# The triangular solve of a DeltaNet stage kept on VectorE, with the steps around it placed anew

## The chip, the cores and the metric

The kernel runs on one core of a Trainium2 chip. The metric is the device time of one execution in microseconds. TensorE (PE; PEld its weight loads), VectorE (DVE), ScalarE (ACT), GpSimd (POOL) and SyncE (SP, which here only issues DMA transfers) run their own instruction streams and meet at semaphores. L282 means line 282 of the kernel before.

## The reference

One layer of a hybrid trunk, on 2048 prompt frames of one stream and on 8 sample streams of 16 frames, with a model width of 1024, all in float32:

```
h   = RMSNorm(x);  P = h @ w_in      -> q|k|v (3*512) | z 512 | b 4 | a 4 | B 512 | C 512 | H 512
A   (gated DeltaNet, 4 heads x 128): causal conv(4) + SiLU on q,k,v; l2norm q,k; beta = sigmoid(b)
    g = -exp(A_log) softplus(a + bias);  decay[i,j] = exp(G_i - G_j), i >= j, G = cumsum(g) in a chunk
    A = strict(beta k k^T * decay);  solve (I + A) [u | w] = [beta v | beta k exp(G)]   (unit lower triangular)
    v_new = u - w S;  o = (q exp(G)) S + (q k^T * decay) v_new;  S = S a_last + k_tail^T v_new
    o = RMSNorm_head(o) * SiLU(z)
B   (short conv): y = B * conv3(C * H)
x   = x + RMSNorm(concat(o, y) @ w_o);  x = x + RMSNorm(SwiGLU(RMSNorm(x)))
```

The order of frames binds two things: the convolution's history, and the state S from chunk to chunk. The sample streams bring their own states and depend on no prompt frame.

## The kernel before

Frames are cut into 17 tiles of 128: 16 of the prompt, and tile 16, the sample (8 streams of 16). Every float32 product is made of three matmuls of rounded halves (hi*hi, lo*hi, hi*lo), so a block of the w_in product with its eight k-slices takes 24 matmuls.

**Stage 1** runs to 1065 us. `GROUPS` (L31) orders the tiles in five groups of 3, 4, 4, 3 and 3. Each group goes through 28 *slots*, one for each 128 columns of w_in, in the order of `SEQ` (L40): k, q, two of v, z, two of v, then the C, H and B columns of the short convolution. A slot's 24 matmuls (L282) have up to 512 columns and are issued in three *thirds* (k 0 to 2, 3 to 5, 6 and 7), so 9, 9 and 6 matmuls. After a slot, `finish_block` (L338) reads the PSUM bank: copy (L290), convolution by multiply-adds on VectorE (L286, the "taps"), Silu on ScalarE (L319). For k, q and v a `later` is returned: the turn (transposition by TensorE, L326) of the Silu's output, which the loop at L902 issues at the end of the next slot.

Between thirds, `plan` (L749) places the steps of the DeltaNet at numbered thirds 0 to 83. It counts time with `THIRD`, an assumed length of a third, so `after(us)` is a number of thirds. In order: `gate_rates`, `gate_sums` and `gate_decay` make the cumulated decay, and gate_decay sends it through DRAM (`grow`) to be broadcast, adds the masks (L493) and takes the Exp; `key_norms`; `decay_scale` (L499); `pair_keys` (L511: four k k^T products into a `gbank`, times `dt`, into `AU`, L516); `pair_queries`; `solve_load`, `solve` in four parts, `solve_store`; `level_a` to `level_d`, which join the inverted 32x32 blocks to 128x128 by small matmuls; then the sample's heads or `chunk`, one thread of four steps per prompt tile, that updates S. The next group's x is brought in meanwhile: `x_rows` (sums of squares), `x_norm` (L233: load and scale), `x_split` (hi and lo, L207, L208), the last two k-slices behind the last slot (`next_rows`, L807).

**The triangular solve.** Each tile and head has four diagonal 32x32 blocks. `solve_load` (L525) writes them to DRAM (`sa`) and reads them so that one partition holds one whole block: 48 or 64 partitions, 1024 numbers each (`As`), with an identity in `Ts`. `solve` makes 31 steps, each a product of a column and a row (L546) and a subtraction (L548). `solve_store` writes the inverse (`sT`) and its turned copy (L553, `sU`) to DRAM and reads both back as `td` and `ud` (one tile, `utd`) with a block's rows over partitions. `level_a` starts with ScalarE copies of `ud` (L566) and matmuls on `td` (L573).

TensorE's order is that of the program text (`manual_schedule`, L815); the other engines' instructions are ordered by the framework's scheduler by its own cost model. `issue_after(x)` makes an instruction be issued behind x. SP's queue carries the loads of weights and x in order. In group 0 (and for a quarter of the blocks in group 1) weights come raw and are split: ScalarE rounds (L260), then VectorE or GpSimd subtracts (L262), and the split weights are written to DRAM (`wsplit`) for the later groups. PSUM has eight banks: three for blocks (`dbank`), two for turns (`tbank`), two for small products (`gbank`), one for outputs (`obank`).

**Then**, from L935, w_o is loaded and split, `o_tile` (L940, matmuls L958) makes the mixer's output tile by tile, and the feed-forward network follows (L1174, L1332).

```
            for slot, j in enumerate(SEQ):
                ...
                for s, ks in enumerate((range(0, 3), range(3, 6), range(6, 8))):
                    ...
                    for f in events.pop(3 * slot + s, ()):
                        f()
                while laters:
                    laters.pop()()
                if later:
                    laters.append(later)
```

## Time and profile before

| what | value |
|---|---|
| time, median of 3 runs (lowest to highest) | 2675.58 us (2666.0 to 2676.9) |
| profiled execution: time, span | 2681.41 us, 2679.5 us |
| granted TensorE clock, mean | 0.971 |
| busy: TensorE, VectorE, ScalarE, GpSimd | 2505.2, 1681.2, 981.9, 647.1 us |
| stage 1, windows from 7.57 to 1069.35 | 1061.78 us, TensorE busy 927.34 |

The page's first part gives each engine's busy time and share of the span; its PEclk line gives, for 40 equal slices, the granted clock in tenths of full speed. Windows are rows of "start:end length, busy time (number of instructions) of PE, PEld, DVE, ACT, POOL, granted clock, DMA share, GB/s". Rows of waits read "engine, its output and line <- engine, output and line that it waited for: us in total, times, longest". Rows of the timeline read "start, length, engine, line, operation, output <- inputs, shape, count", with the idle time before them in brackets. Rows of groups end in the total, the mean in ns, and the idle time before them by what ended it. Pieces of the chain of waits read "start, length, what".

### The profile page before, as it was taken

The page shows a single profiled execution, that of the slowest core. Times are in us where ns is not written, and L with a number is a line of the kernel's source. Part 1 is how long each engine was busy: PE and PEld are TensorE (multiplying, and loading weights), DVE is VectorE, ACT ScalarE, POOL GpSimd, SP SyncE. Part 2 cuts the span into 40 slices and gives each one's busy share as a digit, 9 for nine tenths or more (in the row PEclk, how much of TensorE's full clock was granted, in tenths as well). Part 3 has the DMA queues.
Part 4 walks back from the last instruction along what each step waited for, and adds up shares of the span by engine and source line. Part 5 has one row for each costly group of instructions (what it writes and reads, how often), then busy time and mean ns, then how long its engine had stood idle before and what let it go on. Part 6 is the DMA issues. An engine that isn't in the chain of part 4 may idle for free.

```text
span 2679.5 us, 39414 instructions
## 1 busy us (share of the span) xinstructions
PE 2505.2 (93%) x14366; PEld 2281.7 (85%) x14366; DVE 1681.2 (63%) x3081; ACT 981.9 (37%) x2090; POOL 647.1 (24%) x710
## 2 busy tenths in 40 slices
PE   6879989889898888999999999999999999999998
PEld 6777778668798788888999999999999988788876
DVE  5856655554473554585988884454655554677588
ACT  5433522522432522353443442222433335333343
POOL 2321101101010100021655630000000015555564
PEclk8989999999999999999999999999999999999999
DMA  5676555454566565666987888878888954333466
GB/s 199 210 240 205 172 197 192 148 156 171 177 217 210 172 201 183 204 214 218 334 290 261 267 282 264 266 250 257 278 279 282 288 174 129 118 121 122 132 202 189
DMA packets 314993, 567.28 MB, mean 212 GB/s; under 512 B 53564, under 2 KB 201216, under 8 KB 297776
## 3 DMA queue, kind: packets, MB, share of 16 engines
q1 hardware_dynamic: 184384, 487.32, 54.9%
q10 hardware_dynamic: 130416, 77.45, 9.5%
q8 instruction: 113, 1.85, 0.3%
q14 instruction: 80, 0.66, 0.1%
HBM read 402.65 MB, written 162.05 MB: 211 GB/s over the span
## 4 chain that ended last, share of the span: by engine, by line
PE 53%; DVE 6%; DMA 4%; issue 2%; ACT 1%; POOL 1%; ACTq 0%; SPq 0%; DVEq 0%; POOLq 0%
PE fbank L1174 30%; PE fbank L1332 12%; PE dbank L282 3%; PE tbank L958 3%; PE dbank L958 3%; DMA dr<-in_w_dn 1%; DVE acc L1291 1%; DMA partd<-pt 1%; POOL dw L1031 1%; DVE xr L1351 0%; PE ftbank L981 0%; DVE fw L1150 0%; DVE dw L1031 0%; DMA fh<-hTd 0%; DMA ru<-in_w_gu 0%
## 5 line engine op out<-in xcount | busy, mean ns | idle before, releaser
L1174 PE MATMUL fbank<-xh,fw 128*128 128x384 f32 (+1 forms) x3696 | 899.7, 327 | 7.6 <-ACT m L1208 4.0
L282 PE MATMUL dbank<-hi,w 128*128 128x384 f32 (+1 forms) x2240 | 691.2, 377 | 20.6 <-ACT hi L207 12.7
L1174 PEld LDWEIGHTS fbank<-xh,fw 128*128 128x128 f32 x3696 | 651.9, 188 | 9.4 <-ACT m L1208 4.7
L1174 PE MATMUL fbank<-xl,fw 128*128 128x384 f32 (+1 forms) x1848 | 603.0, 326 | 0.0
L282 PEld LDWEIGHTS dbank<-hi,w 128*128 128x128 f32 x2240 | 431.4, 196 | 60.4 <-ACT hi L207 15.1
L1332 PE MATMUL fbank<-dw,as 128*128 128x512 f32 x1980 | 462.3, 395 | 8.9 <-DVE as L1316 2.6
L1332 PEld LDWEIGHTS fbank<-dw,as 128*128 128x128 f32 x1980 | 373.0, 189 | 97.8 <-DVE acc L1291 4.0
L282 PE MATMUL dbank<-lo,w 128*128 128x384 f32 (+1 forms) x1120 | 414.0, 370 | 3.9 <-DVE lo L208 3.9
L1174 PEld LDWEIGHTS fbank<-xl,fw 128*128 128x128 f32 x1848 | 347.7, 188 | 0.0
L1316 POOL TENSOR_TENSOR as<-ar,as 128x256 fp32r<-128x256 f32 (+1 forms) x207 | 186.3, 911 | 282.6 <-ACT as L1313 281.9
L282 PEld LDWEIGHTS dbank<-lo,w 128*128 128x128 f32 x1120 | 220.1, 196 | 24.4 <-DVE lo L208 8.0
L1291 DVE TENSOR_TENSOR acc<-acc,fbank 128x512 f32<-128x512 f32 x248 | 166.4, 682 | 97.4 <-PE fbank L1332 79.6
L1031 POOL TENSOR_TENSOR dw<-dr,dw 128x512 fp32r<-128x512 f32 x52 | 77.3, 1498 | 484.5 <-ACT dw L1029 484.2
L1313 ACT CAST as<-ar 128x256 fp32r<-128x256 f32 (+1 forms) x288 | 118.4, 427 | 188.7 <-PE fbank L1332 134.7
L286 DVE SCALAR_TENSOR_TENSOR acc<-R,cw,acc 128x512 f32<-128x512 f32 (+2 forms) x180 | 122.4, 682 | 68.1 <-ACT acc L315 66.2
L1149 ACT CAST fw<-rg 128x512 fp32r<-128x512 f32 x124 | 77.4, 624 | 192.3 <-PE fbank L1174 148.5
L1221 DVE TENSOR_TENSOR c<-u,fbank 128x384 f32<-128x384 f32 (+1 forms) x66 | 34.9, 528 | 102.0 <-PE fbank L1174 101.9
L307 POOL COPY hist<-R 128x3 f32<-128x3 f32 x60 | 16.3, 271 | 282.8 <-ACT R L290 256.4
L1217 DVE TENSOR_TENSOR m<-m,m 128x384 f32<-128x384 f32 (+1 forms) x44 | 23.1, 526 | 94.5 <-ACT m L1210 94.4
L1219 ACT ACTIVATE m<-fbank 128x384 f32<-128x384 f32 (+1 forms) x66 | 31.3, 474 | 125.0 <-PE fbank L1174 115.8
L1150 POOL TENSOR_TENSOR fw<-rg,fw 128x512 fp32r<-128x512 f32 x44 | 69.6, 1582 | 30.2 <-ACT fw L1149 30.0
L260 ACT CAST w<-wr 128x512 fp32r<-128x512 f32 x70 | 40.3, 617 | 79.0 <-PE dbank L282 49.4
(341 smaller groups left out, 3572.3 us busy)
## 6 DMA issues: line engine op xcount, KB each, us to landing
w<-wsplit SPq DMA_DIRECT2D x105, 1024.0 KB, 5.0
fw<-fsplit SPq DMA_DIRECT2D x188, 512.0 KB, 4.9
fsplit<-fw SPq DMA_DIRECT2D x94, 512.0 KB, 4.2
partd<-pt ACTq DMA_DIRECT2D x88, 384.0 KB, 6.5
rg<-in_w_gu SPq DMA_DIRECT2D x62, 512.0 KB, 3.7
wsplit<-w SPq DMA_DIRECT2D x28, 1024.0 KB, 5.4
ar<-partd SPq DMA_DIRECT2D x48, 384.0 KB, 3.3
wr<-in_w_in SPq DMA_DIRECT2D x70, 256.0 KB, 4.8
```

What stands on the lines that cost most here:

```text
L260: A.copy(wh[:, c], wr)
L282: T.matmul(ps[:, :c], l[:, k, :], r[k][:, :c], start=(k == 0 and r is hi and l is wh), stop=(k == KD - 1 and l is wl))
L286: V.scalar_tensor_tensor(acc, raw(d), w[:, d:d + 1], acc, op0=ALU.mult, op1=ALU.add)
L958: T.matmul(pss[n], m_[:, j, :], w_[k][:, n * 512:(n + 1) * 512], start=(k == 0 and ci == 0), stop=(k == KD - 1 and ci == 2))
L1031: e.tensor_tensor(out=w[:, 1], in0=v, in1=w[:, 0].bitcast(F32), op=ALU.subtract)
L1149: A.copy(w[:, 0], v)
L1150: e.tensor_tensor(out=w[:, 1], in0=v, in1=w[:, 0].bitcast(F32), op=ALU.subtract)
L1174: T.matmul(ps, w_[:, c], b_[k][:, :hw], start=(first and k == 0 and ci == 0), stop=(k == KH - 1 and ci == 2), skip_group_check=not first)
L1291: V.tensor_add(dst, dst, ps)
L1313: ins = A.copy(a[:, 0, :n], v)
L1316: e.tensor_tensor(out=a[:, 1, :n], in0=v, in1=a[:, 0, :n].bitcast(F32), op=ALU.subtract)
L1332: T.matmul(ps, a[:, x_, q * P:(q + 1) * P], w[:, y_], start=(start and q == 0 and ci == 0), stop=(q == c - 1 and ci == 2), skip_group_chec ...
```

## The change

- The sample moves from the first group to the fourth; the groups' sizes stay 3, 4, 4, 3, 3. `x` transposed is laid out in the groups' order. In `SEQ`, all z columns come ahead of all v columns.
- The solve stays on the chip. `solve_load` gathers the diagonal blocks with four ScalarE copies into `pk`, and one VectorE transposition of 32x32 squares spreads them in `As` so that each block lies on two partitions, each of which holds one half of the inverse's columns (the even or the odd ones). `Ts` gets a constant half identity by one DMA. A step works on 128 partitions and on j // 2 + 1 columns where it had j + 1. `solve_store` makes `td` and `ud` with two VectorE transpositions. All transfers by `sa`, `sT` and `sU` are gone.
- The decay of all tiles is one buffer with one broadcast DMA; the masks are a step of their own, `decay_mask`, issued behind the taps issued latest (`mark["V"]`), with one Exp for all tiles. The sigmoid's Exp moves from `gate_rates` into `gate_sums`, next to the other Exps.
- `laters` are issued one third of a slot later: behind the first third of the slot after the next.
- `THIRD` and the distances in `plan` are changed; chunks begin at third 52 at the earliest (54 before), the sample's heads follow each other by 5 thirds (6 before).
- Loads of x are steps of their own (`x_rows_load`, `x_load`), ahead of the arithmetic; the slices for k = 6 and 7 have buffers of their own and are loaded at thirds 72 and 73.
- Of the second halves of the raw weights VectorE splits the first eight only, GpSimd the others.
- In the last group `ahead`, at third 64, loads two blocks of w_o and the first tile's mixer input into buffers that are free by then, and the first `o_tile` starts from them.

The diff, cut to its core. Where a function is listed above, lines taken out of it are left out here if the new ones replace them whole.

```diff
-GROUPS = [[0, 1, 16], [2, 3, 4, 5], [6, 7, 8, 9], [10, 11, 12], [13, 14, 15]]
+GROUPS = [[0, 1, 2], [3, 4, 5, 6], [7, 8, 9, 10], [11, 12, 16], [13, 14, 15]]
...
-THIRD = {3: 1.75, 4: 2.35}
+THIRD = {3: 1.95, 4: 2.5}
...
-SEQ = [*range(0, 4), *range(8, 12), 4, 5, *range(12, 16), 6, 7, *range(16, 28)]
+SEQ = [*range(0, 4), *range(8, 12), *range(12, 16), *range(4, 8), *range(16, 28)]
...
+    e = np.arange(512)[None, :]
+    c[:, 904:1416] = e // 16 == 2 * (e % 16) + i[:, None] // 16 % 2
...
-        def x_rows(tiles, i, nx):
+        def x_rows_load(tiles, i, nx):
             if not i:
                 nx["ss"] = small.tile([P, 2 * MAXT], F32, tag="xss", name="xss")
+            nx["xt"] = []
             for q in range(2):
+                xt = cp.tile([P, W1], F32, tag="x", name="xt")
                 with tc.issue_after(wloads[-1].ins):
                     nc.sync.dma_start(out=xt, in_=x[tiles[i], :, q * 512:(q + 1) * 512])
+                nx["xt"].append(xt)
+        def x_rows(i, nx):
+            for q, xt in enumerate(nx["xt"]):
                 acc = nx["ss"][:, q * MAXT + i:q * MAXT + i + 1]
+                with tc.issue_after(mark["V" if q else "A"].ins):
+                    if q:
+                        V.scalar_tensor_tensor(xt, xt, 1.0, xt, op0=ALU.mult, op1=ALU.mult, accum_out=acc)
+                    else:
+                        A.activation(xt, xt, AF.Square, accum_out=acc)
...
+        def x_load(tiles, k, nx):
+            c, (gi, _) = len(tiles) * P, PLACE[tiles[0]]
+            xk = xbuf() if k < KD - 2 else cp.tile([P, W1], F32, tag="x", name="xt")
+            o = sum(len(g) for g in GROUPS[:gi]) * P
+            with tc.issue_after(wloads[-1].ins):
+                nc.sync.dma_start(out=xk[:, :c], in_=xT[k, :, o:o + c])
+            nx["xk"].append(xk)
         def x_norm(tiles, k, nx):
+            c, xk = len(tiles) * P, nx["xk"][k]
+            with tc.issue_after(mark["V"].ins):
+                V.tensor_mul(xk[:, :c], xk[:, :c], nx["rb"][:, :c])
...
+        wlo = [0]
...
                 A.copy(wh[:, c], wr)
+                e = V if q and wlo[0] < 8 else G
+                wlo[0] += q
                 e.tensor_tensor(out=wl[:, c], in0=wr, in1=wh[:, c].bitcast(F32), op=ALU.subtract)
...
+            mark["A"] = A.activation(dst[:, :pc], acc[:, :pc], AF.Silu)
...
+                mark["A"] = A.activation(g["sz"][:, h, :c], src, AF.Silu)
...
+            gg = sm("gg")
...
             V.tensor_mul(v3(gg)[:, :n], sp3[:, :n, 4:8], nega.unsqueeze(1).broadcast_to([P, n, H]))
+            g["sp3"], g["gg"] = sp3, gg
...
             m = 4 * n
             V.tensor_scalar_mul(nG[:, :m], ps[:, :m], -1.0)
             V.tensor_add(tl[:, :m], ps[:, 64:64 + m], nG[:, :m])
+            with tc.issue_after(A.activation(tl[:, :m], tl[:, :m], AF.Exp).ins):
+                A.activation(eG[:, :m], ps[:, :m], AF.Exp)
+                A.activation(eL[:, :m], ps[:, 64:64 + m], AF.Exp)
+                if g["npr"] < n:
+                    g["eLs"] = sm("eLs", 4 * NS)
+                    A.activation(g["eLs"], ps[:, 128:128 + 4 * NS], AF.Exp)
+                sb = sm("sb")
+                A.activation(sb[:, :m].rearrange("p (t h) -> p t h", h=H), g["sp3"][:, :n, 0:4], AF.Exp, scale=-1.0)
+            g.update(nG=nG, eG=eG, tl=tl, eL=eL, beta=sb)
...
             nc.scalar.dma_start(out=grow[:m], in_=rw[:m])
...
+            g["dt"] = dt = gp.tile([P, MAXT, H, P], F32, tag="dt", name="dt")
+            nc.sync.dma_start(out=dt[:, :n].rearrange("p t h c -> p (t h) c"), in_=grow[:m].partition_broadcast(P))
+        def decay_mask(g):
+            dt, nG = g["dt"], g["nG"]
+            with tc.issue_after(mark["V"].ins):
+                for i, t in enumerate(g["tiles"]):
+                    for h in range(H):
+                        V.scalar_tensor_tensor(dt[:, i, h, :], dt[:, i, h, :], nG[:, 4 * i + h:4 * i + h + 1],
+                                               neg_s if t == SAMPLE else neg_p, op0=ALU.add, op1=ALU.add)
+            A.activation(dt[:, :g["n"]], dt[:, :g["n"]], AF.Exp)
         def decay_scale(g, i):
...
         def solve_load(g):
+            n = g["n"]
+            As, Ts = (wk.tile([P, NS * (P + LS)], F32, tag=nm, name=nm) for nm in ("As", "Ts"))
+            Ts = Ts[:, :512]
+            nc.sync.dma_start(out=Ts, in_=half_eye)
+            pk = wk.tile([P, H, P], F32, tag="kl", name="pk").rearrange("p h c -> p (h c)").rearrange("p (i x) -> p i x", i=32)
+            if n < MAXT:
+                G.memset(pk, 0.0)
+            if g["npr"] < n:
+                G.memset(U[:, g["npr"]], 0.0)
             for b in range(4):
                 r = slice(32 * b, 32 * b + 32)
+                A.copy(pk[r, :, :4 * n], AU[r, :n, :, r].rearrange("p t h i -> p i (t h)"))
+            As = As[:, :1024].rearrange("p (j i) -> p j i", j=32)
+            V.transpose(As.rearrange("p j i -> p i j"), pk.unsqueeze(2).broadcast_to([P, 32, 2, 4 * MAXT]))
+            g.update(As=As, Ts=Ts.rearrange("p (i c) -> p i c", i=32))
         def solve(g, js):
-            m, As, Ts = g["n"] * 16, g["As"], g["Ts"]
+            As, Ts = g["As"], g["Ts"]
             for j in js:
                 pr = wk.tile([P, 256], F32, tag="pr", name="pr")
-                a, b = 31 - j, j + 1
-                p3 = pr[:m, :a * b].rearrange("p (i c) -> p i c", c=b)
-                V.tensor_mul(p3, As[:m, j, j + 1:32].unsqueeze(2).broadcast_to([m, a, b]),
-                             Ts[:m, j, 0:b].unsqueeze(1).broadcast_to([m, a, b]))
-                V.tensor_sub(Ts[:m, j + 1:32, 0:b], Ts[:m, j + 1:32, 0:b], p3)
+                a, b = 31 - j, j // 2 + 1
+                p3 = pr[:, :a * b].rearrange("p (i c) -> p i c", c=b)
+                V.tensor_mul(p3, As[:, j, j + 1:32].unsqueeze(2).broadcast_to([P, a, b]),
+                             Ts[:, j, 0:b].unsqueeze(1).broadcast_to([P, a, b]))
+                V.tensor_sub(Ts[:, j + 1:32, 0:b], Ts[:, j + 1:32, 0:b], p3)
         def solve_store(g):
             utd = wk.tile([P, NS * (P + LS)], F32, tag="As", name="utd")
+            ud, td = (utd[:, 512 * q:512 * q + 512].rearrange("p (x c) -> p x c", c=32) for q in range(2))
+            V.transpose(td.rearrange("p x (k e) -> p k e x", e=2), g["Ts"].rearrange("p i c -> p c i"))
+            V.transpose(ud, td)
+            g.update(ud=ud.rearrange("p (t h) c -> p t h c", h=H), td=td.rearrange("p (t h) c -> p t h c", h=H))
...
-            third = THIRD[n]
+            third = THIRD[n] if gi else 2.3
...
-            at(5 + after(11), gate_sums, g)
-            at(5 + after(16), gate_decay, g)
-            tk = 15
-            at(tk, key_norms, g)
+            t = 5 + after(11)
+            at(t, gate_sums, g)
+            t += after(4.5)
+            at(t, gate_decay, g)
+            t = max(t + after(12), 17)
+            at(t, decay_mask, g)
+            at(17, key_norms, g)
+            t += after(6)
...
-                at(tk + after(3), decay_scale, g, i)
-                at(tk + after(7 + 2 * i), pair_keys, g, i)
+                at(t - 1, decay_scale, g, i)
+                at(t + after(2 * i), pair_keys, g, i)
                 at(33 + 2 * i, pair_queries, g, i)
-            t = tk + after(8 + 2 * n)
+            t += after(2 * n + 2)
             at(t, solve_load, g)
-            t += after(8)
+            t += after(4)
             for b in range(4):
-                at(t + after(6 * b), solve, g, range(8 * b, min(31, 8 * b + 8)))
-            t += after(25)
+                at(t + after(5 * b), solve, g, range(8 * b, min(31, 8 * b + 8)))
+            t += after(22 if gi else 28)
             at(t, solve_store, g)
-            t += after(16)
+            t += after(4)
             for f in (level_a, level_b, level_c, level_d):
...
                 t += after(3.4)
-            t = max(t + 1, 54)
+            t = max(t + 1, 52)
             hop = after(3.6)
...
-                    u = t + 1 + 6 * h
+                    u = t + 1 + 5 * h
                     thread((u, u + 3, u + 5, u + 7, u + 9), sample_head(g, npr, h))
                 at(u + 10, lambda: out_norm(g, npr, smp["o"]))
-                at(u + 15, lambda: out_turn(g, npr, smp["o"]))
+                at(u + 14, lambda: out_turn(g, npr, smp["o"]))
             for i in range(npr):
...
+                m = len(tiles)
+                for i in range(m):
+                    at(44 + 3 * i, x_rows_load, tiles, i, nx)
+                    at(47 + 3 * i - (i < m - 1), x_rows, i, nx)
+                at(48 + 3 * m, x_spread, tiles, nx)
+                ts = [62, 65, 68, 69, 70, 71, 72, 73]
+                for k in range(KD):
+                    at(ts[k], x_load, tiles, k, nx)
+                    if k < NHX:
+                        at(ts[k] + 3, x_norm, tiles, k, nx)
+                        at(ts[k] + 4, x_split, tiles, k, nx)
+                    else:
+                        at(ts[k] + 4, x_norm, tiles, k, nx)
+            else:
+                at(64, ahead, g)
+        def ahead(g):
+            kt, vt, sz = (g[nm][:, :, MAXT - 1] if nm != "sz" else g[nm][:, :, W1 - P:] for nm in ("kt", "vt", "sz"))
+            early_w[:] = [(U[:, MAXT - 1], AU[:, MAXT - 1]), (g["dt"][:, MAXT - 1], kt)]
+            for k, halves in enumerate(early_w):
+                for q, v in enumerate(halves):
+                    nc.sync.dma_start(out=v, in_=w_o[k, :, 512 * q:512 * q + 512].rearrange("p (h c) -> p h c", h=H))
+            early_m[:] = [vt, sz]
+            nc.sync.dma_start(out=vt, in_=mixo[0])
+            gi, i = PLACE[0]
+            nc.sync.dma_start(out=sz, in_=mixs[gi][:, :, i * P:(i + 1) * P])
...
             for k in range(NHX, KD):
-                if k >= KD - 2:
-                    x_norm(tiles, k, nx)
                 x_split(tiles, k, nx)
...
+                    while s == 0 and len(laters) > 1:
+                        laters.pop(0)()
                     for f in events.pop(3 * slot + s, ()):
                         f()
-                while laters:
-                    laters.pop()()
-                if later:
-                    laters.append(later)
+                laters.append(later or (lambda: None))
...
         for k in range(KD):
-            wr = op.tile([P, D], F32, tag="xo", name="wor", bufs=2)
-            nc.sync.dma_start(out=wr, in_=w_o[k])
             wh = oa.tile([P, D], F32R, name=f"woh{k}")
             wl = oa.tile([P, D], F32R, name=f"wol{k}")
-            A.copy(wh, wr)
-            V.tensor_sub(wl, wr, wh.bitcast(F32))
+            if k < len(early_w):
+                for q, v in enumerate(early_w[k]):
+                    a, b = (h4(w[:, 512 * q:512 * q + 512]) for w in (wh, wl))
+                    A.copy(a, v)
+                    V.tensor_sub(b, v, a.bitcast(F32))
+            else:
+                wr = op.tile([P, D], F32, tag="xo", name="wor", bufs=2)
+                nc.sync.dma_start(out=wr, in_=w_o[k])
+                A.copy(wh, wr)
+                V.tensor_sub(wl, wr, wh.bitcast(F32))
...
         def o_tile(t):
+            if t == 0:
+                mr = early_m
+            else:
+                m = oa.tile([P, KD, P], F32, tag="mr", name="mr")
+                mr = m[:, 0:4], m[:, 4:8]
+                nc.sync.dma_start(out=mr[0], in_=mixo[t])
+                gi, i = PLACE[t]
+                nc.sync.dma_start(out=mr[1], in_=mixs[gi][:, :, i * P:(i + 1) * P])
...
+    a["xT"] = np.concatenate([xt[:, :, t * P:(t + 1) * P] for g in GROUPS for t in g], axis=2)
+    a["xs0"] = a["xT"][:, :, :len(GROUPS[0]) * P]
...
```

98 lines of the change are left out of this document (18 added, 80 removed).

## The prediction, made before the result was known

> **What bounds the kernel now.** I read the page's first two parts, then the span cut at the five groups, then TensorE's waits, then the clock beside single waits.
>
> ```profile
> span 2679.5 us, 39414 instructions
> PE 2505.2 (93%) x14366; PEld 2281.7 (85%) x14366; DVE 1681.2 (63%) x3081; ACT 981.9 (37%) x2090; POOL 647.1 (24%) x710
> PEclk8989999999999999999999999999999999999999
> ```
>
> TensorE is 93% busy over the span, so time can come from two places only: its idle time and its clock. The diff reaches only to the first `o_tile` (L958, 1065 us). The windows are: weights arriving, then groups 0 to 4.
>
> ```profile
> core 0: us, PE busy (x) PEld busy (x) DVE busy (x) ACT busy (x) POOL busy (x), PEclk, DMA share, GB/s
> 32.00:252.00 220.00, 180.87 (x1128) 169.94 (x1126) 153.17 (x351) 86.11 (x179) 54.47 (x74) 0.89 0.63 210
> 252.00:478.00 226.00, 205.75 (x1256) 170.17 (x1255) 134.83 (x281) 83.83 (x162) 32.85 (x51) 0.97 0.54 185
> 478.00:707.00 229.00, 204.01 (x1244) 169.17 (x1244) 118.33 (x259) 71.88 (x141) 20.71 (x43) 0.96 0.49 164
> 707.00:884.00 177.00, 157.03 (x1086) 150.64 (x1086) 95.32 (x227) 62.77 (x125) 18.14 (x40) 0.94 0.61 203
> 884.00:1069.35 185.35, 160.28 (x1114) 154.00 (x1115) 96.19 (x227) 64.09 (x133) 16.65 (x38) 0.94 0.55 181
> sum 1061.78, PE 927.34 PEld 828.87 DVE 612.93 ACT 378.97 POOL 150.97; mean PE 154.56 PEld 138.14 DVE 102.16 ACT 63.16 POOL 25.16
> ```
>
> So 1061.78 - 927.34 = 134 us of stage 1 are idle, and the clock column adds more: group 0 and group 3 have three tiles each, and group 0, which holds the sample, takes 43 us longer for 42 more matmuls, at 0.89. TensorE's waits up to 1100 us say for whom:
>
> ```profile
> engine line waited for: us in total, times, longest us
> PE gbank L573 <- DMA utd<-sT: 52.2, 5, 13.5
> PE tbank L326 <- ACT qT L319: 28.2, 9, 4.9
> PE dbank L282 <- ACT hi L207: 12.7, 5, 4.7
> PE tbank L326 <- ACT kT L319: 11.7, 9, 3.1
> PE tbank L326 <- ACT vraw L319: 8.4, 5, 3.8
> PE dbank L958 <- ACT mh L952: 7.0, 1, 7.0
> PE dbank L282 <- DVE lo L208: 3.9, 8, 1.1
> PE gbank L716 <- POOL R L305: 3.8, 1, 3.8
> ```
>
> Five times, once a group, `level_a` waits for the solve's blocks (52.2 us); 23 times a turn (transpose) waits for a Silu (28.2 + 11.7 + 8.4 = 48.3). Windows cut just behind a wait give the clock's part; the sum row is that of the five windows behind `level_a`, the first of which is shown, and the last two rows stand behind turns that had waited 1.83 and 1.87 us.
>
> ```profile
> 160.89:164.82 3.93, 3.93 (x41) 3.87 (x42) 0.69 (x1) 2.88 (x7) 0.94 (x2) 0.50 0.02 4
> ...
> sum 22.65, PE 22.64 PEld 21.08 DVE 2.57 ACT 15.39 POOL 3.63; mean PE 4.53 PEld 4.22 DVE 0.51 ACT 3.08 POOL 0.73
> ...
> 724.60:728.02 3.42, 3.42 (x13) 3.42 (x12) 1.94 (x4) 3.38 (x6) 0.00 (x0) 0.50 0.48 204
> 554.25:558.00 3.75, 3.75 (x19) 3.19 (x20) 3.68 (x10) 1.01 (x2) 0.19 (x1) 1.00 0.57 238
> ```
>
> After each `level_a` wait TensorE works at half rate: 22.65 us, half of it lost, 11.3. After a turn's wait it sometimes does (3.42 us, 1.7 lost), sometimes not.
>
> **The solve.** Rows of group 1: last AU product, first step, copy between the transfers, and `level_a`, with the steps' spread.
>
> ```profile
> 311.08 0.69 DVE L516 TENSOR_TENSOR AU<-gbank,dt 128x512 f32<-128x512 f32 x1
> ...
> 321.58 0.18 DVE L546 TENSOR_TENSOR pr<-As,Ts 64x31 f32<-64x31 f32 x1 [2.92 <-DMA As<-sa]
> 321.79 0.21 DVE L548 TENSOR_TENSOR Ts<-Ts,pr 64x31 f32<-64x31 f32 x1
> ...
> 355.26 1.12 DVE L553 COPY As<-Ts 64x1024 f32<-64x1024 f32 x1
> ...
> 354.69 0.61 PE L282 MATMUL dbank<-hi,w 128*128 128x512 f32 x2
> ...
> 355.38 0.61 PE L282 MATMUL dbank<-hi,w 128*128 128x512 f32 x2
> ...
> 368.18 0.75 PE L573 MATMUL gbank<-utd,AU 32*32 32x32 f32 x20 [9.02 <-DMA utd<-sT]
> 366.46 2.50 ACT L566 COPY U<-utd 32x512 f32<-32x512 f32 x4 [2.88 <-DMA utd<-sU]
> L546 DVE TENSOR_TENSOR pr<-As,Ts x31: 183/349/416, 321.6 to 354.8; 64x31 f32<-64x31 f32 x2, 64x60 f32<-64x60 f32 x2, 64x87 f32<-64x87 f32 x2, 64x112 f32<-64x112 f32 x2
> L548 DVE TENSOR_TENSOR Ts<-Ts,pr x31: 181/359/1444, 321.8 to 355.0; 64x31 f32<-64x31 f32 x2, 64x60 f32<-64x60 f32 x2, 64x87 f32<-64x87 f32 x2, 64x112 f32<-64x112 f32 x2
> ```
>
> From AU's end (311.8) to `level_a` 56 us pass: 9.8 of transfers, 33.7 of solve with other VectorE work between, 1.1 of copy, 11.8 of transfers. Both transfer legs go. A step takes 183 ns at 31 elements a partition and 416 ns at 256, hence 0.15 us + 1.04 ns an element. The 62 instructions of a group hold 10912 elements now (20.7 us), 5712 afterwards (15.3), and some 0.035 us between two makes 17.5. Around them come four ScalarE copies (2.5 by L566), one transposition of 1024 elements (1.1, as L553) and two of 512 (0.6 each): 22.3 us alone, and 27 to 33 with 5 to 11 us of taps between, where now 10.7 lie (33.7 less 20.7 and 2.3). Against it stands what TensorE has to do from the last `pair_keys` to `level_a`: in the built program 114 block matmuls in groups 1 and 2, three in 0.69 us from 354.69 to 355.38, so 26, plus query products and turns, 29.5; in the three-tile groups 153 to 159, about 30.5. Left over per group are 0 to 3.5 us, say 9.5 in all, and 3.5 of half clock. Saved: 52.2 + 11.3 - 13 = **50 us**. On SP's queue a group loses five transfers (`As`, `sT`, `sU`, `utd` twice) and gains one, the constant half identity into `Ts`, which nobody needs before the first step; ScalarE's queue loses four issues and gains the copies; POOL gains a memset of `pk` and one of `U`'s sample part where three tiles are, off the path at 16 to 54 us busy a group.
>
> No row shows a VectorE transposition. Lower end: the copy's 2.3 us a group; it can't be much below, as the elements are the same. Upper end: the slowest L548 took 1444 ns where the median is 359, four times as much, so 9.2 us, 7 more a group, 35 in all. I take the copy, the nearest row. [...]
>
> **Turns a third later.** `laters` now runs after the next slot's first third: 9 more matmuls of cover, 2.05 us at 512 columns (three in 0.69) and 1.55 at 384. Two things shorten the Silu's path besides:
>
> ```profile
> L319 ACT ACT_TABLE_LOAD x24 | 30.8, 1283 | 7.8 <-DVE ssk L504 3.1 <-DVE acc L286 2.6 <-DVE rw L484 1.7
> L493 DVE SCALAR_TENSOR_TENSOR dt<-dt,nG,cst 128x128 f32<-128x128 f32 x68 | 19.5, 349 | 7.5 <-DMA dt<-grow 7.3
> L499 DVE TENSOR_TENSOR dt<-dt,c 128x512 f32<-128x512 f32 x17 | 12.6, 781 | 0.0
> L262 POOL TENSOR_TENSOR w<-wr,w 128x512 fp32r<-128x512 f32 x35 | 46.7, 1334 | 90.0 <-ACT w L260 89.9
> L262 DVE TENSOR_TENSOR w<-wr,w 128x512 fp32r<-128x512 f32 x35 | 32.3, 922 | 5.9 <-ACT w L260 5.7
> ```
>
> Grouped Exps spare 17 table loads at 1.28 us in stage 1, and the masks (12 or 16 x 0.35 us) are issued behind the taps. The mean wait is 48.3/23 = 2.1 us. About 13 us of the 48.3 stay (group 0, where weights are split, and the longest, 4.9 - 2.05 - 1.28 = 1.6 each). Half clock: between nothing and 23 x 1.7 = 39, I take the middle, 20, of which half goes: 35 + 10 = **45 us**. [...]
>
> **Changeovers and the end.**
>
> ```profile
> 878.70 5.56 DMA xk<-in_xT
> ...
> 1056.40 6.90 DMA wor<-in_w_o
> ```
>
> x for k = 6, 7 is requested only behind the last slot, and the hi/lo pair (12.7 + 3.9 us) waits. Afterwards it lies in buffers of its own, asked for at thirds 72 and 73 of 84, with 20 us of cover; norm and split can still be late. Saved with its half clock (three of 1.7): **16**. At the end the first two w_o blocks and tile 0's mix are loaded ahead, so the 6.90 transfer leaves the path; what is late next is w_o block 2, still requested there, and of 7.0 I count **4**. The sample's wait on POOL (3.8) moves with it to group 3; its heads follow every 5 thirds instead of 6: **1.6**. The weight split moved from VectorE to GpSimd, copies to ScalarE (37% busy) and the loads on SP's queue count nothing: block k is requested several slots ahead; without that cover each block would lose 1.33 - 0.92 = 0.4 us per half moved (the two L262 rows), 11 us for the 27 halves.
>
> **What is new.** `pair_keys` is planned at slot 7 behind one Exp over all tiles, which waits for the masks (16 x 0.35 = 5.6 us at most, less where nothing disturbs them) and is followed by four scalings (4 x 0.78). There are two gbanks, so the third product waits until VectorE has read the first: I count 4 to 4.7 us in groups 1 and 2, 1.3 in group 0, with half clock 13 together. From below nothing (Exp ready in time), from above the `level_a` wait of today, about 10 in each of five groups, 50. I take 13, nearer to the chain's own terms. For waits of chunks from third 52 instead of 54, sample heads and first o tile: 10 (between 0 and the 20 that twelve waits of 1.7 would cost).
>
> **Sum.** 50 + 45 + 16 + 4 + 1.6 - 13 - 10 = 93.6. The profiled execution took 2681.41 us, 1.9 above its span, and lies 5.8 above the median, 2675.58. Taken from the median: **2582 us**.
>
> **Rivals.**
> *The solve stays late:* transpositions or taps stretch VectorE's chain by 7 us a group; TensorE waits it out, 35 us plus half clock of 8: 2625. For it: group 0's VectorE is busy 153 of 220 us. Against: the chain has lost 21 us of transfers.
> *The gbank takes over:* the third `pair_keys` waits as `level_a` does, 50 instead of 13: 2619. For it: L499 and the masks stand in front of it on one engine. Against: it is one link, not a round trip.
> *Nearly everything goes:* chain inside the cover, turns free: 13 + 13 + 10 + 10 less lost: 2545 to 2555. For it, 134 us idle plus clock in stage 1 leave room.
> *The change doesn't do what it says:* the waits shortened at one step come back at the next, because each engine keeps one order and TensorE's next input is behind the same taps: no change, 2675. Against: VectorE is busy only 613 of 1062 us.
> *Slower:* a VectorE transposition works in pieces. It decides when a group's three cost 21 us instead of 2.3, as 5 x 18.7 eats 93.6; at 30 us a group VectorE's chain would be 28 longer, 138 us: 2720. For it: nothing but that no row shows one; against: the slowest VectorE row above is four times its kind, this would be nine.
>
> **How the numbers follow.** Forecast (2560 to 2608) 0.53; nearly everything 0.14; late solve 0.11; gbank 0.10; no change 0.03; slower 0.09, the single mechanism with whatever else ends there. 8 in 10: 2545 to 2640. A difference under about 0.5% (13 us) can't be told from none. Faster 0.88, same 0.03, slower 0.09.
>
> **What would show it.** `level_a` waits on VectorE, not a transfer, under 4 us each; As and Ts steps at 128 partitions with 15 to 18 us a group; a transposition near 1.1 us; turn waits below 15 us; gbank waits at `pair_keys` in slot 7; L958 waiting about 3 us instead of 7; windows of groups near 195, 210, 210, 165, 165. Wrong would be: VectorE above 75% in group windows, or new waits over 25 us.

## The result, and the profile after

The changed kernel takes **2584.05 us** (median of 4 runs, 2578.59 to 2594.55) against 2676.24 for the kernel before beside it: a ratio of 0.9665, with a 95% interval of 0.962 to 0.9711, so 92 us less. The forecast was 2582.

The changed kernel's own four executions lie 16 us apart, at mean granted clocks of 0.981 to 0.988; the profiled one (2589.22 us) is the second longest.

The first two lines of the page of the changed kernel:

```profile
span 2587.4 us, 39334 instructions
PE 2487.6 (96%) x14366; PEld 2271.3 (88%) x14366; DVE 1669.2 (65%) x3044; ACT 978.7 (38%) x2095; POOL 687.0 (27%) x741
```

TensorE has as many matmuls as before and a larger share of a shorter span. Where the time went is read by cutting both kernels at the first product on w_o. First the kernel before, then the changed one, each one window (columns as in the prediction):

```profile
0.00:1065.01 1065.01, 923.01 (x5886) 825.32 (x5886) 611.95 (x1371) 380.12 (x760) 151.77 (x261) 0.94 0.57 190
```

```profile
0.00:974.68 974.68, 905.81 (x5890) 814.85 (x5890) 600.93 (x1335) 376.87 (x766) 192.12 (x292) 0.97 0.58 202
```

Stage 1 is 90.3 us shorter, so the rest of the kernel gives 1.8 of the 92. The work on TensorE is the same (5886 and 5890 matmuls recorded), so its busy time should shrink only through the clock: 923.0 - 905.8 = 17 us, and idle time goes from 142.0 to 68.9, 73 us. The trace bears this out. TensorE was busy for 86.6 us in the half-rate stretches of stage 1 before and for 51.3 after. In both traces products of 128x512 on w_in start 0.43 us apart in such stretches and 0.23 apart at full rate (medians), so about half of that busy time is lost; by the clock of 0.50 it is 43.3 and 25.7, which is 17.6 less. All runs below are read by these two numbers, idle and busy time.

The windows of the changed kernel by group, cut at its own boundaries:

```profile
32.00:211.80 179.80, 154.45 (x1044) 148.15 (x1044) 133.82 (x262) 83.21 (x163) 79.34 (x84) 0.91 0.65 224
211.80:418.70 206.90, 201.87 (x1245) 168.56 (x1244) 129.00 (x262) 83.52 (x158) 41.80 (x58) 0.98 0.54 192
418.70:619.60 200.90, 198.32 (x1245) 166.16 (x1244) 116.89 (x262) 73.89 (x140) 21.61 (x45) 1.00 0.52 181
619.60:814.10 194.50, 177.10 (x1166) 168.09 (x1165) 113.58 (x301) 64.64 (x158) 22.09 (x52) 0.95 0.60 204
814.10:977.30 163.20, 155.70 (x1115) 150.51 (x1114) 92.05 (x224) 58.48 (x122) 16.56 (x37) 0.98 0.58 202
```

Groups 1 and 2 are now close to full: 202 of 207 and 198 of 201 us busy, at a clock of 0.98 and 1.00. Group 0 is not (154 of 180, at 0.91), nor group 3, which now holds the sample. TensorE's waits of the changed kernel up to 1100 us:

```profile
PE gbank L538 <- DVE AU L539: 11.5, 3, 6.3
PE gbank L593 <- DVE utd L578: 11.0, 3, 5.2
PE gbank L736 <- DMA st<-in_state: 8.3, 2, 4.8
...
PE tbank L345 <- DVE R L311: 5.3, 1, 5.3
PE tbank L345 <- ACT qT L338: 4.9, 4, 3.2
...
PE dbank L1008 <- ACT mh L1002: 3.7, 1, 3.7
PE tbank L345 <- ACT kT L338: 2.8, 3, 2.2
...
PE gbank L593 <- issue: 1.1, 1, 1.1
```

`level_a` (now L593) waits for VectorE, no longer for a transfer: 52.2 us became 11.0 + 1.1. The turns (L345) went from 48.3 to 5.3 + 4.9 + 2.8 = 13.0. The waits for hi and lo (L300) went from 16.6 to 2.6 (1.5 + 1.1, rows not shown). New are the third `pair_keys` (L538, 11.5) and the sample's states (L736, 8.3).

The solve's instructions in the changed kernel, by line (count: least/median/greatest ns, first and last start):

```profile
L560 ACT COPY pk<-AU x20: 830/880/1130, 80.5 to 868.8; 32x384 f32<-32x384 f32 x12, 32x512 f32<-32x512 f32 x8
L562 DVE STREAM_TRANSPOSE As<-pk x5: 1925/2087/2109, 84.0 to 869.7; 128x1024 f32<-128x1024 f32 x5
L578 DVE STREAM_TRANSPOSE utd<-Ts x5: 1059/1073/1141, 122.3 to 898.8; 128x512 f32<-128x512 f32 x5
L579 DVE STREAM_TRANSPOSE utd<-utd x5: 698/711/714, 124.9 to 899.9; 128x512 f32<-128x512 f32 x5
L571 DVE TENSOR_TENSOR pr<-As,Ts x155: 168/267/1398, 87.7 to 898.4; 128x126 f32<-128x126 f32 x15, 128x30 f32<-128x30 f32 x10, 128x56 f32<-128x56 f32 x10, 128x78 f32<-128x78 f32 x10
```

The three transpositions take 2.09 + 1.07 + 0.71 = 3.9 us a group, between the forecast's ends of 2.3 and 9.2; the four copies take 3.5 instead of 2.5. The steps (L571 and its subtraction, L573) take 93.2 us in five groups, 18.6 each, where 15.3 were put and 21.6 were taken before.

### The profile page after: what moved, and what is told of

It is laid out like the page before. It is cut to its first block, busy times and chain, and to the rows that moved or that the text cites. A ratio compares the mean times of both kernels' runs of the same rounds, so it can differ in the third digit from the quotient of the medians.

```text
span 2587.4 us, 39334 instructions
## 1 busy us (share of the span) xinstructions
PE 2487.6 (96%) x14366; PEld 2271.3 (88%) x14366; DVE 1669.2 (65%) x3044; ACT 978.7 (38%) x2095; POOL 687.0 (27%) x741
## 4 chain that ended last, share of the span: by engine, by line
PE 77%; DVE 12%; DMA 4%; ACT 3%; issue 2%; POOL 1%; ACTq 0%; SPq 0%; DVEq 0%; POOLq 0%
PE fbank L1224 33%; PE dbank L300 20%; PE fbank L1382 11%; PE tbank L1008 3%; PE dbank L1008 3%; DVE Ts L573 1%; DVE pr L571 1%; DVE acc L304 1%; DVE acc L1341 1%; PE gbank L736 1%; PE tbank L345 1%; DMA dr<-in_w_dn 1%; DMA partd<-pt 1%; DVE xr L1401 1%; PE gbank L688 1%
## 5 line engine op out<-in xcount | busy, mean ns | idle before, releaser
L300 PE MATMUL dbank<-hi,w 128*128 128x384 f32 (+1 forms) x2240 | 681.3, 372 | 9.1 <-ACT w L277 7.6
L300 PEld LDWEIGHTS dbank<-hi,w 128*128 128x128 f32 x2240 | 423.8, 193 | 47.6 <-ACT w L277 7.6
L300 PE MATMUL dbank<-lo,w 128*128 128x384 f32 (+1 forms) x1120 | 407.7, 364 | 1.5 <-DVE lo L213 1.5
L300 PEld LDWEIGHTS dbank<-lo,w 128*128 128x128 f32 x1120 | 216.0, 193 | 21.2 <-DVE lo L213 4.1
L304 DVE SCALAR_TENSOR_TENSOR acc<-R,cw,acc 128x384 f32<-128x384 f32 (+2 forms) x180 | 129.0, 719 | 64.9 <-ACT acc L334 58.6
L280 POOL TENSOR_TENSOR w<-wr,w 128x512 fp32r<-128x512 f32 x62 | 86.7, 1413 | 60.0 <-ACT w L277 49.9
L1200 DVE TENSOR_TENSOR fw<-rg,fw 128x512 fp32r<-128x512 f32 x80 | 56.4, 706 | 15.6 <-ACT fw L1199 13.2
```

What stands on the lines that cost most here:

```text
L280: e.tensor_tensor(out=wl[:, c], in0=wr, in1=wh[:, c].bitcast(F32), op=ALU.subtract)
L300: T.matmul(ps[:, :c], l[:, k, :], r[k][:, :c], start=(k == 0 and r is hi and l is wh), stop=(k == KD - 1 and l is wl))
L304: r = V.scalar_tensor_tensor(acc, raw(d), w[:, d:d + 1], acc, op0=ALU.mult, op1=ALU.add)
L1200: e.tensor_tensor(out=w[:, 1], in0=v, in1=w[:, 0].bitcast(F32), op=ALU.subtract)
```

## The experiments

Every ratio is to the kernel before on the same chip. Stage 1 is the time of the first product on w_o in the profiled execution, idle and busy are TensorE's times up to there, in us.

| run | ratio (95%) | stage 1 | idle | busy |
|---|---|---|---|---|
| before | 1 | 1065.0 | 142.0 | 923.0 |
| changed | 0.9665 (0.962 to 0.9711) | 974.7 | 68.9 | 905.8 |
| solve_only | 0.9884 (0.9863 to 0.9905) | 1028.5 | 110.9 | 917.6 |
| solve_turns | 0.975 (0.9723 to 0.9778) | 996.6 | 84.0 | 912.7 |
| three | 0.9671 (0.9651 to 0.969) | 974.9 | 69.5 | 905.4 |
| turns_old | 0.9742 (0.9716 to 0.9768) | 990.9 | 84.9 | 906.0 |
| x_late | 0.9801 (0.9777 to 0.9825) | 1006.7 | 87.8 | 918.9 |
| pk_later | 0.9708 (0.9686 to 0.973) | 985.5 | 79.1 | 906.4 |
| split_alt | 0.9671 (0.965 to 0.9691) | 969.0 | 65.7 | 903.4 |
| masks_free | 0.9682 (0.9654 to 0.9711) | 978.9 | 72.9 | 906.0 |
| sample_first | 0.965 (0.9626 to 0.9674) | 965.4 | 64.3 | 901.1 |
| no_ahead | 0.9717 (0.9694 to 0.974) | 978.1 | 74.2 | 904.0 |
| relaxed | 0.9612 (0.9593 to 0.9631) | 958.6 | 62.0 | 896.6 |

The changed kernel and the runs were timed on different chips, each beside the kernel before, and the changed kernel's interval is the widest. By the two intervals together, differences of less than some 13 us between it and a run can't be told by the ratios alone. The waits and the idle time of the profiled executions are then the better witness, though each is of one execution.

**Building up from the kernel before.** *solve_only* takes over `solve_load`, `solve`, `solve_store` and the half identity, and nothing else; the nine transfers a group go (in part):

```diff
-            g["sa"], g["sT"], g["sU"] = (dram.tile([MAXT, H, 4, 32, 32], F32, name=f"{nm}{gi}") for nm in ("sa", "sT", "sU"))
...
+                A.copy(pk[r, :, :4 * n], AU[r, :n, :, r].rearrange("p t h i -> p i (t h)"))
...
+            V.transpose(As.rearrange("p j i -> p i j"), pk.unsqueeze(2).broadcast_to([P, 32, 2, 4 * MAXT]))
...
+            V.transpose(td.rearrange("p x (k e) -> p k e x", e=2), g["Ts"].rearrange("p i c -> p c i"))
+            V.transpose(ud, td)
```

> The kernel before with the solve kept on the chip and nothing else changed, the plan's thirds as they were (they leave room for both transfer legs). Theory: the five waits of level_a (52.2 us) and the half clock behind them (11.3) vanish altogether: 55 to 65 us less than before, about 2615. Rival: VectorE's chain with the taps between is what is late, not the transfers: a wait of 4 us or more stays in most groups, and the gain is 35 us or less.

Measured: 31 us less, not 60. TensorE's waits:

```profile
PE tbank L329 <- ACT qT L322: 47.1, 13, 6.9
...
PE tbank L329 <- ACT kT L322: 11.4, 9, 3.1
PE tbank L329 <- ACT vraw L322: 8.5, 2, 6.8
...
PE gbank L588 <- issue: 0.8, 1, 0.8
PE gbank L588 <- ACT xs L574: 0.2, 1, 0.2
```

Neither theory held as written. `level_a` (here L588) lost its whole wait, 52 to 1 us, as the theory said, so the transfers were what was late there. But the turns of q now wait 13 times and 47.1 us, where they waited 9 times and 28.2. Of 51 us of wait that left `level_a`, 19 came back at the q turns.

Almost all of it (18.4 us) lies in one turn of each group, which waits 2.5 to 7.0 us now (1.6 before in group 0, nothing in the others) and ends its wait 2.4 to 5.7 us behind the solve's first step. These are rows of group 1, on three engines:

```profile
305.16 4.48 ACT L538 COPY pk<-AU 32x512 f32<-32x512 f32 x4
309.67 0.59 ACT L293 COPY R<-dbank 128x512 f32<-128x512 f32 x1
309.67 2.09 DVE L540 STREAM_TRANSPOSE As<-pk 128x1024 f32<-128x1024 f32 x1 [4.55 <-ACT pk L538]
...
315.63 0.63 ACT L322 ACTIVATE qT<-acc 128x512 f32<-128x512 f32 x1 [4.17 <-DVE acc L289]
316.32 0.66 PE L329 MATMUL tbank<-cst,qT 128*128 128x128 f32 x4 [2.54 <-ACT qT L322]
```

q's block is finished by 307.7, but its copy out of PSUM (L293) stands behind the solve's four copies on ScalarE until 309.67. On VectorE the transposition, and then steps of the solve, stand ahead of and between q's taps, which start at 311.91. So the Silu is late by both engines; no run takes one of the two away by itself.

*solve_turns* adds the turns a third later:

```diff
+                    while s == 0 and len(laters) > 1:
+                        laters.pop(0)()
...
+                laters.append(later or (lambda: None))
```

> The kernel before with the solve on the chip and, besides, the turns a third of a slot later; nothing else changed. With the solve alone the level_a waits went from 52 to 1 us but the waits of the q turns rose from 28 to 47, and only 31 us of about 60 were gained. Theory (the wait moved: taps and Silus now stand behind the solve's steps on VectorE, and a turn a third later covers that): the turn waits fall from 67 below 35 and the time by a further 25 to 45 us, to 2600 to 2620. Rival: the turns' waits are longer than a third, so most of each stays; less than 15 us are gained.

Measured: 0.975, a further 36 us, in the theory's range. The waits:

```profile
PE tbank L329 <- ACT qT L322: 30.8, 9, 5.6
...
PE tbank L329 <- ACT vraw L322: 7.0, 4, 4.2
...
PE tbank L329 <- ACT kT L322: 2.0, 4, 1.0
```

The turns' waits fall from 67.0 to 39.8, so they stay above the 35 expected, and still the whole time falls by as much as was expected. Idle time fell by 27, and busy time by 5 more.

*three* adds x for k = 6 and 7 in buffers of its own, requested at thirds 72 and 73 and scaled at 81 and 82:

```diff
+                for k in (KD - 2, KD - 1):
+                    at(72 + k - KD + 2, x_early, tiles, k, nx)
+                    at(81 + k - KD + 2, x_norm, tiles, k, nx)
```

> The kernel before with three parts of the change: the solve on the chip, the turns a third later, and x for k = 6 and 7 requested early (thirds 72 and 73, scaled at 81 and 82). Theory: these three make the change, and the rest (groups, sequence, masks, grouped Exps, weight split, distances, loads ahead) is worth under 10 us together: 15 to 32 us less than with the first two, 2578 to 2595. Rival: the rest carries 15 us or more, and this kernel stays above 2598.

Measured: 0.9671, the changed kernel's time. Solve, turns and early x, added in this order, make 31 + 36 + 21 us; everything else in the change nets to less than can be told (1.6 us by the ratios). It does move waits, though. The waits of *three*:

```profile
PE tbank L341 <- ACT qT L334: 30.7, 9, 5.7
...
PE tbank L341 <- ACT vraw L334: 7.0, 4, 4.2
...
PE dbank L297 <- ACT hi L210: 2.7, 2, 1.4
...
PE tbank L341 <- ACT kT L334: 2.0, 4, 1.0
```

Here the turns wait 39.7 us and `pair_keys`, `level_a` and the states hardly at all; in the changed kernel the turns wait 13.0, and those three 11.5 + 12.1 + 8.3 = 31.9. So the rest of the change, masks, grouped Exps, sequence and tighter distances together, took some 27 us of wait from the turns and put 32 at the products. Of these four only the masks were tried alone (*masks_free*, below).

**Taking parts out of the changed kernel.** *turns_old* puts the turns back to the end of the next slot:

```diff
-                    while s == 0 and len(laters) > 1:
-                        laters.pop(0)()
...
+                while laters:
+                    laters.pop()()
```

> The changed kernel with the turns of k, q and v issued again at the end of the next slot, all else as changed. Theory (the forecast's second term): the 9 matmuls of cover were worth most of the turns' saving, so TensorE's waits at the turns go from 13 us back towards 48 and the time rises by 25 to 40 us against the changed kernel. Rival: the masks behind the taps and the spared table loads did it, and the waits stay below 25 us; the time rises by less than 12 us.

Measured: 0.9742, some 20 us slower, between the two. The waits at the turns are 11.3 for q, 10.9 for v and 10.7 for k, 32.9 together against 13.0. So of the 35 us by which the change shortened the turns' waits, 20 are the later turn, and the rest is what came with it.

*x_late* requests x for k = 6 and 7 behind the last slot:

```diff
-                for k in range(KD):
+                for k in range(KD - 2):
                     at(ts[k], x_load, tiles, k, nx)
...
+                if k >= KD - 2:
+                    x_load(tiles, k, nx)
+                    x_norm(tiles, k, nx)
```

> The changed kernel with x for k = 6 and 7 requested again only behind a group's last slot. Theory: the waits for hi and lo at the four changeovers come back, 12 to 17 us of wait with 3 to 5 of half clock: 12 to 20 us slower than the changed kernel. Rival: the transfer was hidden by the chunks' work or by the order of the loads: under 5 us.

Measured: 0.9801, 36 us slower, nearly twice the theory's upper end. The waits are what was expected, the clock is not. The wait of the changeovers in the whole-stage list and, below it, the four stretches behind them (first and last shown, and the sum row of the four windows):

```profile
PE dbank L300 <- ACT hi L212: 19.0, 5, 6.1
...
219.20:226.00 6.80, 6.12 (x14) 3.02 (x15) 3.45 (x5) 3.50 (x6) 1.22 (x2) 0.50 0.00 0
843.90:850.70 6.80, 3.59 (x10) 2.48 (x11) 2.35 (x4) 2.10 (x4) 0.19 (x1) 0.50 0.31 106
sum 23.80, PE 17.77 PEld 9.76 DVE 9.76 ACT 9.19 POOL 1.78; mean PE 4.44 PEld 2.44 DVE 2.44 ACT 2.30 POOL 0.44
```

Idle time rose by 18.9 us and busy time by 13.1. Each of the four waits, 3.3 to 6.1 us, comes with a half-rate stretch, 17.8 us busy together, half of which is lost: 8.9. All half-rate stretches of stage 1 cost 36.3 us here and 25.7 in the changed kernel, so 10.6 of the 13.1 are clock; the other 2.5 aren't explained.

*no_ahead* drops the loads ahead:

```diff
-            else:
-                at(64, ahead, g)
```

> The changed kernel without the loads ahead of the first w_o blocks and of the first tile's mixer input. Theory (the forecast's 4 us): the first product on w_o waits 7 us again instead of 3.7, and the time rises by 3 to 6 us. Rival: hidden, within 2 us.

Measured: the first product on w_o waits 9.7 us instead of 3.7 and starts 3.5 later (978.1 against 974.7), and the profiled execution is 3.5 longer, in the theory's range. The ratio, 0.9717, says 14 us, with an interval that overlaps the changed kernel's. That the wait is 6 us shorter with the loads ahead is shown; whether the time gains 3.5 us or more stays open.

*split_alt*, *masks_free* and *sample_first* undo one thing each:

```diff
-                e = V if q and wlo[0] < 8 else G
+                e = V if q else G
...
-            with tc.issue_after(mark["V"].ins):      # in decay_mask
...
-GROUPS = [[0, 1, 2], [3, 4, 5, 6], [7, 8, 9, 10], [11, 12, 16], [13, 14, 15]]
+GROUPS = [[0, 1, 16], [2, 3, 4, 5], [6, 7, 8, 9], [10, 11, 12], [13, 14, 15]]
```

> The changed kernel with every second half of the raw weights split on VectorE again instead of the first eight only (27 halves of 0.92 us go back to VectorE, off GpSimd at 1.4). Theory: VectorE is what sets the pace in group 0 (134 of 180 us busy), so 25 us of work there cost 5 to 15 us. Rival: while GpSimd subtracts, VectorE's own instructions take up to 1.4 us instead of 0.27, so the move saved VectorE nothing: the same within 4 us, or faster.

> The changed kernel with the masks of the decay no longer held behind the latest taps: the scheduler may put them ahead. Theory: the Exp comes earlier and the third pair_keys no longer waits for its bank (11.5 us), but taps, Silus and turns come later by 4 to 5 us in slot 6 or 7 of each group: within 8 us of the changed kernel, with the waits moved from pair_keys to the turns. Rival: the placing behind the taps was worth most of the turns' saving: 15 us slower or more.

> The changed kernel with the groups as before: the sample in the first group, the prompt's tiles shifted. The forecast priced the move at 1.6 us. Theory: group 0 is short of VectorE time already, and the sample brings it longer taps and its own work, so the time rises by 8 to 20 us against the changed kernel. Rival: the sample's waits for its states (8 us) and for POOL simply move with it: the same within 5 us.

Measured: 0.9671, 0.9682 and 0.965, all the changed kernel's time within what can be told. For the weight split the rival holds: group 0 doesn't need VectorE's time back (how long VectorE's instructions took beside GpSimd's is in the last section). For the masks the first theory holds: the L538 wait is gone (11.5 to 0), and q's turns wait 13.0 instead of 4.9 and `level_a` 16.1 (10.2 + 5.9) instead of 12.1. For the sample the rival holds, and the place of the sample is worth nothing that shows; its profiled stage 1 is even 9 us shorter.

**Moving waits.** *pk_later* moves `pair_keys` and what follows two thirds back in groups 0 to 2, and `level_a` one more third in groups 1, 3 and 4:

```diff
-            t += after(6)
+            t += after(6 if gi > 2 else 12 if gi else 10)
...
-            t += after(4)
+            t += after(4 if gi == 0 or gi == 2 else 6)
```

> The changed kernel with pair_keys and all behind it two thirds later in groups 0 to 2, and level_a one third later in groups 1, 3 and 4. Theory: the third pair_keys product waits for VectorE to have read the first one's bank because the Exp comes late (11.5 us in three groups), and level_a waits on VectorE's chain (12 us): both shrink, 10 to 20 us less than the changed kernel. Rival: the wait moves along, since VectorE's order puts the same work ahead of the same product: within 5 us of the changed kernel, or slower where chunks start later.

Measured: 0.9708, 11 us slower by the ratio, with intervals that overlap, and 10 us more idle: the rival. The L538 wait is gone altogether, but group 0 alone (window 32 to 211) has these instead:

```profile
PE gbank L593 <- issue: 8.8, 1, 8.8
PE tbank L345 <- ACT qT L338: 8.6, 2, 8.4
PE tbank L345 <- ACT vraw L338: 5.4, 1, 5.4
PE obank L659 <- DVE o L654: 4.3, 2, 3.2
```

```profile
98.00:135.90 37.90, 22.00 (x126) 21.05 (x124) 36.49 (x86) 10.76 (x22) 15.84 (x18) 0.91 0.69 239
```

The second fence is the window of *pk_later* in which group 0's steps run: VectorE is busy 36.5 of 37.9 us while TensorE is busy 22. The solve now shares VectorE with the taps of v, and `level_a`, placed as close as before, waits 8.8 us for the last transposition. (The profile calls that wait "issue"; the transposition before it on VectorE ends at 135.84, and L593 starts at 135.94.)

*relaxed* leaves `pair_keys` and the solve alone, and moves `level_a` back by 3, 1, 1, 2 and 2 thirds and the sample's heads apart again:

```diff
-            t += after(4)
+            t += after(4) + (3, 1, 1, 2, 2)[gi]
...
-                    u = t + 1 + 5 * h
+                    u = t + 1 + 6 * h
```

> The changed kernel with level_a three thirds later in group 0, one in groups 1 and 2, two in groups 3 and 4 (pair_keys and the solve stay), and the sample's heads 6 thirds apart instead of 5. Theory: the level_a waits (12 us) and the waits for the sample's states (8 us) have slack to go into, since the chunks keep their pace: 10 to 22 us less than the changed kernel. Rival: as with pair_keys moved later, the waits come back at other steps (chunks bunched towards the end of the group): within 5 us, or slower.

Measured: 0.9612, 2572.03 us, 12 to 14 us less than the changed kernel: the theory, though the two intervals just touch. Beside *three*, which ran on the same chip and takes the changed kernel's time, it is 16 us less, with intervals apart. This is the fastest version run. Its waits:

```profile
PE gbank L538 <- DVE AU L539: 11.5, 3, 6.3
PE obank L659 <- DVE o L654: 10.9, 4, 7.4
...
PE gbank L593 <- DVE utd L578: 3.7, 3, 2.6
PE gbank L736 <- DVE st L756: 1.7, 1, 1.7
```

`level_a` falls from 12.1 to 3.7 and the states from 8.3 to 1.7; the output turn (L659) takes 6 of the 15 back (4.8 before, 10.9 now). Idle time falls by 7, busy time by 9; half-rate stretches of stage 1 cost 16.1 us here and 25.7 in the changed kernel, so the busy time is the clock that went with the waits.

*transposes* adds eight instructions to scratch, four kinds, each twice (a part of the diff):

```diff
+                flat = g["Ts"].rearrange("p i c -> p (i c)")
...
+                            V.transpose(pr, flat[:, 0:256])
...
+                            V.transpose(pr.rearrange("p (i j) -> p j i", j=8), flat[:, 0:256].rearrange("p (j i) -> p j i", j=8))
...
+                            V.transpose(pr.rearrange("p (j i) -> p j i", j=8), flat[:, 0:256].rearrange("p (i j) -> p j i", j=8))
...
+                            V.tensor_copy(pr, flat[:, 0:256])
```

> The changed kernel with eight more VectorE instructions on 256 elements a partition behind the last group's solve, into scratch that nothing reads: two transpositions from flat to flat, two that write with a stride of 8 elements, two that read with a stride of 8, two plain copies. The trace of the changed kernel has 2.09 us for 1024 elements with strides, 1.07 for 512 with strides, 0.71 for 512 flat. Theory: a stride doubles the time of an element (about 2.0 ns instead of 1.1): 0.4 us flat and 0.6 to 0.7 strided, on whichever side the stride is. Rival: only the written side counts, or the broadcast read did it: the strided read stays near 0.4.

One execution was taken, for its trace. The timeline of VectorE there (the first of the two flat ones, before these rows, also takes 0.41):

```profile
900.78 0.41 DVE L586 STREAM_TRANSPOSE pr_a<-Ts 128x256 f32<-128x256 f32 x1
901.22 1.33 DVE L588 STREAM_TRANSPOSE pr_b<-Ts 128x256 f32<-128x256 f32 x2
902.58 1.33 DVE L590 STREAM_TRANSPOSE pr_c<-Ts 128x256 f32<-128x256 f32 x2
903.95 0.62 DVE L592 COPY pr_d<-Ts 128x256 f32<-128x256 f32 x2
```

Flat to flat takes 0.41, a stride 0.66 whether it is written or read, a copy 0.31: the theory. The two flat sizes, 0.41 and 0.71 us (L579) for 256 and 512, give 1.2 ns an element; the strided ones, 0.66, 1.07 and 2.09 for 256, 512 and 1024, give 1.6 and 2.0. A copy takes 1.05 ns an element (0.31 us for 256 here, 1.12 for 1024 in the prediction's rows). The strided sizes, two of which the change uses, take 1.5 to 1.6 times the flat ones at the same size.

## Why the prediction was right, point by point

**The total** (2582 against 2584) is right, and the way in is right: the end was set by TensorE's idle time and clock in stage 1, and 90 of the 92 us came from there. That it is right to 2 us is partly luck. By the runs in sequence, the terms of solve and turns were 28 us too large (95 against 67) and the changeovers 5 too small (16 against 21); the other terms, put at 17.4 lost in sum, come to 1.6 gained.

**The solve, 50 us.** The wait did fall as summed, 52.2 to 12.1 (9.5 was forecast). But as a part by itself the solve is worth 31 (*solve_only*). The step that was off is that the gain was booked at the place where the wait stood; the work of VectorE and ScalarE came forward and 19 us of wait came up at the q turns. The steps were put at 15.3 us a group and take 18.6; 14 of the 17 us that this makes in five groups are in 16 steps that lie under GpSimd instructions (last section). The terms of solve and turns belong together: 31 + 36 = 67 measured in sequence, 50 + 45 = 95 forecast.

**The transposition's price.** 2.3 us a group was taken, 3.9 measured, between the bounds. The row chosen as nearest, a copy of 1024 elements in 1.12 us, was of the right kind for a flat one (0.71 for 512); strides were not thought of (1.07 for 512, 2.09 for 1024; *transposes*).

**The turns, 45 us.** The remaining wait was put at 13 and is 13.0. Undone in the changed kernel the later turn is worth 20 us, added to the solve 36: its value depends on how much waits there. The 17 spared table loads are there (54 in stage 1 before, 37 after).

**Changeovers, 16 us.** The mechanism is right and the size too small: 21 us in *three*, 36 in *x_late*. The clock behind the waits was booked at 1.7 us each for three; measured are four stretches that cost 8.9 together, 2.2 each.

**The end, 4 us.** L958 (now L1008) waits 3.7 instead of 7.0, as put; *no_ahead* starts the product 3.5 later in its profile.

**The gbank, 13 lost.** 11.5 measured, and in three groups as forecast, though with 6.3 in group 0, where 1.3 was put, and 2.6 each in groups 1 and 2, where 4 to 4.7 were put. Losing it again gains nothing by itself (*masks_free*, *pk_later*).

**The sample, 1.6 gained, and 10 for the unknown.** The wait for the states, 8.3, and for `obank`, 4.8, fill the 10. The windows by group were partly wrong: 165 us were put for group 3 and 194.5 measured, 195 for group 0 and 179.8 measured, as far as can be told because the sample's work was left in group 0. Where the sample stands doesn't matter (*sample_first*).

**The clock.** The half-rate stretches cost 17.6 us less; the forecast's clock terms (11.3 - 3.5 behind `level_a`, 10 at turns, 5 at changeovers, less 3) come to 20.

**The rivals and the signs.** No rival decided. The gbank's and the late solve's mechanisms are there, with 11.5 and 12.1 us in place of 50 and 43, and that of waits that come back at the next step is there in *solve_only*, with 19. The terms of *nearly everything goes*, 46 us, taken from 2582 make 2536 and not 2545 to 2555. Of the signs named, these didn't come: every `level_a` wait under 4 us (5.2 in group 3), steps of 15 to 18 us a group (18.6), a transposition near 1.1 us (2.09 for the one of 1024 elements). VectorE's share stayed just below the 75% named as a sign of being wrong: 133.82 of 179.80 us in group 0, 74%.

## What to carry to other kernels

When a wait is removed on one engine, ask which work of other engines now starts earlier and what stands behind it in their order: here 19 of 51 us came back at the next consumer of the same engines, and moving that consumer too gained another 36. A wait of TensorE cost its own length here and at times clock besides: in *x_late* idle time rose by 18.9 us, with four waits of 3.3 to 6.1 (17.7 together), and 10.6 more were lost at half rate, so these waits were worth more than their sum. Here a chain ended late against a consumer that was placed tightly: putting the consumer later (*relaxed*) gained 12 to 14 us, while putting the producer later (*pk_later*) pushed it among other work, and TensorE was idle for 10 us more.

## What the runs showed of the hardware

**Which waits cost clock.** In all fourteen traces the recorded granted clock changes only on a fixed grid of 3.41 us, and the half-rate stretches of stage 1 last one to four of its steps (3.41 to 13.65 us). Of the two turns in the prediction that waited about as long, 1.83 and 1.87 us, one was followed by half rate and one was not. The grid steps in which they waited tell them apart (kernel before):

```profile
721.19:724.60 3.41, 1.58 (x11) 1.26 (x10) 1.08 (x7) 3.37 (x6) 0.37 (x2) 1.00 0.43 125
550.52:553.93 3.41, 1.86 (x9) 1.21 (x7) 3.38 (x10) 0.36 (x1) 0.18 (x1) 1.00 0.35 58
```

The first wait (to 723.94) lies in one step and leaves TensorE busy for 46% of it; the next step is at half rate. The second (to 554.25) reaches into the next step and leaves 54%; the next step is at full rate. Counted over the steps between 40 and 960 us of all fourteen traces: of the full-rate steps, all 138 in which TensorE was busy for less than 43% were followed by half rate, 7 of 47 between 43 and 55%, and 7 of 3310 above. Of the half-rate steps, 158 of 168 with 80% or more were followed by full rate, and none of 82 with less. The kernel before and the changed one alone have 25 of 25, 1 of 6, 1 of 459, 28 of 30 and none of 17. So in these traces half rate goes not with a wait's length alone but with how much of one grid step it takes.

**VectorE beside GpSimd.** A VectorE step of the solve at times takes several times as long as others of its shape. In the changed kernel 16 of the 310 steps take over 1.5 times the shortest of their shape, 14 us more in all, and each of the 16 lies under a GpSimd arithmetic instruction of 1.0 us or more, as this one (two of GpSimd's in one row):

```profile
95.92 2.56 POOL L280 TENSOR_TENSOR w<-wr,w 128x512 fp32r<-128x512 f32 x2 [1.90 <-ACT w L277]
95.93 1.40 DVE L571 TENSOR_TENSOR pr<-As,Ts 128x96 f32<-128x96 f32 x1
```

The shortest of this shape takes 0.25 us. Of the other 294 steps, 6 overlap a GpSimd instruction longer than 0.5 us. In *split_alt* it is 11 of 11 slow steps. No run takes GpSimd's work away altogether, and that moving 27 splits off it (*split_alt*, its busy time in stage 1 192 to 155 us) left the time as it was says that it isn't worth much here.
